# Gate products on half the rows of the array, low parts written over their source, and a later scaling in the final norm

## The chip, the cores and the metric

The kernel runs on one core of a Trainium2 chip. The metric is the device time of one launch in microseconds (us). Five engines work side by side, each through its own stream of instructions: TensorE (PE; its weight loads are shown as PEld), VectorE (DVE), ScalarE (ACT), GpSimd (POOL) and SyncE (SP), which issues the DMAs. An engine waits for another through semaphores.

## The reference

One decoder block on 2048 tokens of 1024 channels, all in float32:

```python
u = rms_norm(h, norm1_gain)
x_lru, g_lru, q, k, v, g_ret = split(u @ w_in)                  # 6 x 512 columns
xc = causal_depthwise_conv(x_lru)                               # width 4
r = sigmoid(einsum("bshi,hij->bshj", xc_by_head, wa) + ba)      # 8 heads of 64
i = sigmoid(einsum("bshi,hij->bshj", xc_by_head, wx) + bx)
a = exp(-8 * r * softplus(-lam))
hl = scan(h = a*h + sqrt(1 - a*a) * (i*xc))                     # RG-LRU
y_lru = rms_norm(hl * gelu(g_lru))
y_ret = head_norm(retention(rotary(q), rotary(k), v)) * silu(g_ret)   # 4 heads of 128
h = h + concat(y_lru, y_ret) @ w_out
up = causal_depthwise_conv(rms_norm(h) @ ffn_up_w)              # width 3, 2 x 3072 columns
a_branch, v_branch = split(up)
h = h + (gelu(a_branch) * v_branch) @ ffn_down_w
return rms_norm(h, final_norm_gain)
```

The two einsums are the gates: each of the 8 heads has its own 64x64 matrix for r and another for i.

## The kernel before

Channels lie on partitions and tokens on the free axis. A big product is made in three fp32r products instead of one fp32 product. Each operand x is split into a high part, which ScalarE rounds to fp32r (CAST; `bh` of the data, `wh` of the weights), and a low part x - high, which VectorE subtracts (`bl`, `wl`). TensorE then adds wh·bh + wh·bl + wl·bh. The large matrices are multiplied by a Strassen scheme: a `Unit` takes 2x2 blocks and makes seven products of 12 matmuls of 128x512; the first of the seven factors are sums of weight blocks (`s`, `s1`) that VectorE makes. A `PlainUnit` takes the eight plain products of a 2x2 scheme instead and needs no sums. The kernel has 745 such groups of 12 matmuls ("product blocks"); they fill PSUM banks named pq, px, py, pe.

The work runs in stages for two groups of 1024 tokens, g0 and g1: the input projection of g0 (its first units plain, on raw input, hence `RawStage`; then Strassen units) and of g1, with the gates, the scan and the retention among them until about 610 us; the output projection of both (plain); from about 815 us the up-projection of g0, then of g1, with its width-3 convolution (tiles `c`, `o`); and from about 1735 us the down-projection of both. `Stage.bring` loads a 512 KB block of data into a slot `raw`, splits it into two further slots and frees the raw one. SBUF is cut into 54 slots of 128x1024 floats.

The order of all instructions is worked out ahead by a planner (`Flow`): every piece of work is a Python generator that yields operations with a cost in us, a priority in ticks (one tick is about one product block's place), or a request for a slot or a PSUM bank. At each step the planner gives the engine that is free first the ready operation of best priority. `RESERVE` and `NEAR` hold slots back from work that is not due soon, `BACKLOG` bounds how far DMAs are issued ahead, and `WB`, `LESS`, `XD0`, `RAW` and `STAGE_LEAD` set when weight sums, the conversion of x, the split of blocks and their loads fall due. The engines then run the resulting fixed streams, each in its order.

Four pieces are named below. `LruOut.first` makes the gates of one 128-channel tile (two heads) for 1024 tokens: for each half of 512 tokens an fp32 matmul of the full 128x128 block-diagonal matrix into bank `pa` and another into `pg`, then two sigmoids by ACT. There are 8 such tiles (4 in each group), so 16 pairs of gate products. Banks `sm` (three of them) serve the gates and every other small product: scores `sc`, the retention state `pk`, transposes, row sums `mst` (ones times a sum of squares `sqacc`), broadcasts `pb`. `FinalGroup.piece` closes the last RMSNorm: the last pairs of output tiles arrive in token ranges of 512, 256 and 256 columns; when a range is complete, its power (`rstd`: mst, ms on DVE and POOL, pb, then the copy `rb` by ACT) is worked out, and eight scalings res·gain·rb by DVE follow, each with its output DMA.

Of the kernel before, what the change touches and what calls it, by code (L numbers as in the profile page):

```python
# [30 lines left out]
P = 128  # L31
# [11 lines left out]
RESERVE = 7  # L43
NEAR = 3
BACKLOG = 6.0
# [4 lines left out]
WB = 0  # L50
# [3 lines left out]
LESS = 2  # L54
XSTEP = 6
XD0 = 6
XS = 60
XD = 50
RAW = 4
LEAD = 10  # L60
STAGE_LEAD = 16
# [41 lines left out]
class Engine:  # L103
# [24 lines left out]
    def cost_pe(self, op, n, args, kw):  # L128
        if op == "transpose":
            return 0.13  # L130
        one = max(0.03, 0.0133 + n / 2400)
        return one if args[1].dtype == F32R else 4 * one
# [185 lines left out]
def hymba_block_kernel(ctx: ExitStack, tc: tile.TileContext, xh, xn, win, wout, wup, down, gates, vecs,  # L318
# [30 lines left out]
    def dma(dst, src):  # L349
        n = 1  # L350
        for d in dst.shape:
            n *= d
        return Op("sp", lambda: nc.sync.dma_start(dst, src), ISSUE, parts(dst), parts(src), kb=n / 256)
# [141 lines left out]

    class Stage:
# [19 lines left out]
        def bring(self, name, i, need, start):  # L516
            yield Until(start)
            r = yield Slot("raw")
            yield from self.src.get(r, name, i)
            yield need - 2  # L520
            self.blk[name, i] = yield from split(r, "b")
            free(r)
# [8 lines left out]
    class RawStage(Stage):  # L531
# [6 lines left out]
        def bring(self, name, i, need, start):  # L538
            k, n = int(name[0]) - 1, int(name[1]) - 1
            yield Until(start)  # L540
            r = yield Slot("raw")
            if self.gain is None:
                yield from self.src[2 * k + i].get_half(r, n)
# [4 lines left out]
            if self.gain is None:  # L548
                self.blk[name, i] = yield from split(r, "b")
# [8 lines left out]
            free(r)  # L558
# [483 lines left out]
    class LruOut(PlainOut):  # L1042
# [17 lines left out]
        def first(self):  # L1060
# [13 lines left out]
            gat = e[:, 0:2 * P].rearrange("p (a b) -> p a b", b=P)  # L1074
            yield dma(gat, gates[:, 2 * c:2 * c + 2])
# [4 lines left out]
            for n in range(2):  # L1080
                pa = yield Bank("sm", "pa")
                yield pe.matmul(pa, gat[:, 0], xc[:, half(n)], start=True, stop=True)
                px = yield Bank("sm", "pg")
                yield pe.matmul(px, gat[:, 1], xc[:, half(n)], start=True, stop=True)
                yield a.activation(t[:, half(n)], pa, AF.Sigmoid, bias=col(V_BA + c))
                free(pa)
                yield a.activation(gi[:, half(n)], px, AF.Sigmoid, bias=col(V_BX + c))
                free(px)
# [291 lines left out]
    class FinalGroup(NormGroup):  # L1380
# [6 lines left out]
        def piece(self, m, t, c0, c1):  # L1387
# [7 lines left out]
            if self.count % 2 == 0:  # L1395
                r = yield Slot("rb")
                r = r[:, 0:c1 - c0]
                yield from rstd(self.ss.acc, D, r, c0, c1)
                for k in range(KT):
# [4 lines left out]
        def out(self, k, y, c0, c1):  # L1404
            yield dma(yT[k * P:(k + 1) * P, HT * (NG - 1) + c0:HT * (NG - 1) + c1], y)
# [153 lines left out]
def _layout(inputs):  # L1559
# [26 lines left out]
    gates = np.zeros((P, 8, P), f32)  # L1586
    for c in range(4):
        for i, name in enumerate(("lru_gate_a_w", "lru_gate_x_w")):
# [40 lines left out]
```

## Time and profile before

| | |
|---|---|
| time, median of 3 runs | 2207.14 us (2205.99 to 2207.38) |
| the profiled execution's own time | 2206.14 us |
| its span in the trace | 2204.4 us (1.7 us lie outside it) |
| mean granted TensorE clock | 0.993 of full speed |
| busy: PE, DVE, ACT, POOL | 98%, 80%, 56%, 2% |
| TensorE's idle time in all | 33.7 us, of which 7.3 us stand behind its last instruction |

Busy shares are means over the whole span, and a busy TensorE can still run at half speed, so the idle gaps of TensorE, the engine that ended each, and the granted clock in the stretch behind it say more than the shares. Every operation is recorded by one helper line (L124), so rows are told apart by tile names. A matmul's duration in the trace overlaps that of the next; the distance between two starts is what each takes.

### The profile page before, as it was taken

How to read it: one execution, taken by the hardware profiler on the slowest of the kernel's cores; microseconds unless marked ns; L12 is line 12 of the kernel's file. 1: busy time of each engine (PE TensorE's matmuls, PEld its weight loads, DVE VectorE, ACT ScalarE, POOL GpSimd, SP SyncE). 2: the span in 40 equal slices, each digit the busy share in tenths (PEclk: the TensorE clock that was granted, in tenths of full speed). 3: DMA queues.
4: the chain of work that ended last, by engine and by line, in shares of the span. 5: the costliest groups of instructions: out<-in, count | busy, mean ns of one | idle time of the engine just before them, and what ended most of it. 6: DMA issues, size and time to landing. Idle time of an engine off the chain costs nothing.

```text
span 2204.4 us, 26724 instructions
## 1 busy us (share of the span) xinstructions
PE 2170.5 (98%) x9938; PEld 1793.2 (81%) x9938; DVE 1765.0 (80%) x2228; ACT 1224.0 (56%) x1763; POOL 42.0 (2%) x30
## 2 busy tenths in 40 slices
PE   9999999999999999999999999999999999999997
PEld 7877878888888788888888878888888788888886
DVE  6998888777764688898788897878788887797775
ACT  6674665565732266666666866666667544343441
POOL 0010010000000000000000000000000000000000
PEclk9999999999999999999999999999999999999999
DMA  9955464133664944444233532323236677689762
GB/s 345 358 200 191 124 224 157 60 112 103 204 234 177 376 188 143 169 152 161 90 108 126 210 120 84 122 90 110 96 101 217 246 283 274 226 304 345 274 231 77
DMA packets 140530, 408.36 MB, mean 185 GB/s; under 512 B 15728, under 2 KB 20208, under 8 KB 140400
## 3 DMA queue, kind: packets, MB, share of 16 engines
q1 hardware_dynamic: 140400, 406.65, 52.7%
q8 instruction: 78, 1.28, 0.2%
q14 instruction: 52, 0.43, 0.1%
HBM read 273.16 MB, written 125.04 MB: 181 GB/s over the span
## 4 chain that ended last, share of the span: by engine, by line
PE 93%; DVE 4%; DMA 1%; ACT 1%; issue 1%; POOL 0%; SPq 0%; POOLq 0%; DVEq 0%
PE py L124 33%; PE px L124 22%; PE pe L124 21%; PE pq L124 12%; PE po L124 1%; DMA raw<-in_dram 1%; PE sc L124 1%; PE pt L124 1%; PE pb L124 1%; PE pk L124 1%; PE pa L124 1%; PE pg L124 1%; DVE res L124 1%; PE mst L124 1%; DVE wl L124 0%
## 5 line engine op out<-in xcount | busy, mean ns | idle before, releaser
L124 PE MATMUL py<-bh,wh 128*128 128x512 f32 x728 | 288.1, 396 | 3.9 <-ACT wh L124 3.9
L124 PE MATMUL py<-bh,wl 128*128 128x512 f32 x728 | 285.5, 392 | 4.5 <-DVE wl L124 4.5
L124 PE MATMUL px<-bh,wh 128*128 128x512 f32 x728 | 287.7, 395 | 0.0
L124 PE MATMUL pe<-bl,wh 128*128 128x512 f32 x728 | 283.4, 389 | 1.8 <-DVE bl L124 1.8
L124 PE MATMUL py<-bl,wh 128*128 128x512 f32 x728 | 285.1, 392 | 0.0
L124 PE MATMUL px<-bh,wl 128*128 128x512 f32 x728 | 283.5, 389 | 1.6 <-DVE wl L124 1.6
L124 PE MATMUL pe<-bh,wh 128*128 128x512 f32 x728 | 285.0, 391 | 0.0
L124 PE MATMUL pe<-bh,wl 128*128 128x512 f32 x728 | 283.6, 390 | 0.1
L124 PE MATMUL px<-bl,wh 128*128 128x512 f32 x728 | 283.5, 389 | 0.0
L124 DVE TENSOR_TENSOR wl<-s,wh 128x1024 fp32r<-128x1024 f32 x182 | 222.1, 1220 | 71.3 <-ACT wh L124 71.0
L124 ACT CAST wh<-s 128x1024 fp32r<-128x1024 f32 x182 | 190.6, 1047 | 133.3 <-DVE s L124 119.2
L124 DVE SCALAR_TENSOR_TENSOR c<-o,vec,c 128x1022 f32<-128x1022 f32 x192 | 245.5, 1279 | 14.8 <-ACT c L124 9.3
L124 PE MATMUL py<-bh,wv 128*128 128x512 f32 x728 | 241.5, 392 | 1.0 <-DVE res L124 0.8
L124 ACT COPY o<-py 128x512 f32<-128x512 f32 x204 | 119.9, 588 | 199.5 <-PE py L124 196.4
L124 ACT CAST bh<-raw 128x1024 fp32r<-128x1024 f32 x158 | 162.9, 1050 | 54.7 <-DMA raw<-g 15.0
L124 DVE TENSOR_TENSOR bl<-raw,bh 128x1024 fp32r<-128x1024 f32 x158 | 189.3, 1218 | 4.3 <-ACT bh L124 3.2
L124 ACT ACTIVATE c<-o,vec 128x1024 f32<-128x1024 f32 x96 | 119.7, 1246 | 97.1 <-DVE o L124 95.6
L124 PE MATMUL pq<-bh,wh 128*128 128x512 f32 (+1 forms) x432 | 168.8, 391 | 1.3 <-ACT bh L124 1.2
L124 PE MATMUL pq<-bh,wl 128*128 128x512 f32 (+1 forms) x432 | 165.8, 384 | 1.5 <-DVE wl L124 1.5
L124 PEld LDWEIGHTS py<-bh,wl 128*128 128x128 f32 x728 | 137.7, 189 | 35.1 <-DVE wl L124 6.1
L124 PE MATMUL pq<-bl,wh 128*128 128x512 f32 (+1 forms) x432 | 165.5, 383 | 0.3 <-DVE bl L124 0.3
L124 PEld LDWEIGHTS py<-bh,wh 128*128 128x128 f32 x728 | 137.8, 189 | 33.3 <-ACT wh L124 4.7
(133 smaller groups left out, 3815.6 us busy)
## 6 DMA issues: line engine op xcount, KB each, us to landing
wa<-in_dram SPq DMA_DIRECT2D x91, 512.0 KB, 4.1
wb<-in_dram SPq DMA_DIRECT2D x91, 512.0 KB, 4.7
h<-res SPq DMA_DIRECT2D x56, 512.0 KB, 3.5
g_T<-t SPq DMA_DIRECT2D x96, 256.0 KB, 2.5
raw<-g_T SPq DMA_DIRECT2D x48, 512.0 KB, 6.3
res<-h SPq DMA_DIRECT2D x48, 512.0 KB, 6.2
g<-c SPq DMA_DIRECT2D x76, 256.0 KB, 3.1
raw<-g SPq DMA_DIRECT2D x38, 512.0 KB, 6.4
```

The costliest lines, as they stand in the source:

```text
L124: return Op(self.name, lambda: fn(*args, **kw), us, writes, reads, func=func)
```

## The change

Five edits. The gates of a tile are two products with 64 rows each, the first head's from rows 0 to 63 and the second head's from rows 64 to 127, into two banks, issued as one operation; each bank then holds r of one head and i of the other, and ACT reads four 64-row pieces instead of two of 128 rows. The low part of a data block is written over the raw block, in the slot that the load filled. The final norm's scalings get the lowest priority once the power is known. Half of the last outputs are issued by ACT's queue. Seven of the planner's constants have new values.

```diff
-RESERVE = 7
+RESERVE = 4
-BACKLOG = 6.0
+BACKLOG = 10.0
-WB = 0
+WB = 2
-LESS = 2
+LESS = 0
-XD0 = 6
+XD0 = 10
-RAW = 4
+RAW = 3
-STAGE_LEAD = 16
+STAGE_LEAD = 20
...
         one = max(0.03, 0.0133 + n / 2400)
+        if args[1].shape[0] == 64:
+            one /= 2
...
+    def split_here(raw, name):
+
+        hi = yield Slot(name + "h", F32R)
+        x = raw.bitcast(F32)
+        yield a.copy(hi, x)
+        yield low(raw, x, hi)
+        return hi, raw
...
         def bring(self, name, i, need, start):
             yield Until(start)
-            r = yield Slot("raw")
-            yield from self.src.get(r, name, i)
+            r = yield Slot("raw", F32R)
+            yield from self.src.get(r.bitcast(F32), name, i)
             yield need - 2
-            self.blk[name, i] = yield from split(r, "b")
-            free(r)
+            self.blk[name, i] = yield from split_here(r, "b")
...
-            gat = e[:, 0:2 * P].rearrange("p (a b) -> p a b", b=P)
-            yield dma(gat, gates[:, 2 * c:2 * c + 2])
+            gat = e[:, 0:P]
+            yield dma(gat, gates[:, c])
...
             for n in range(2):
+
                 pa = yield Bank("sm", "pa")
-                yield pe.matmul(pa, gat[:, 0], xc[:, half(n)], start=True, stop=True)
-                px = yield Bank("sm", "pg")
-                yield pe.matmul(px, gat[:, 1], xc[:, half(n)], start=True, stop=True)
-                yield a.activation(t[:, half(n)], pa, AF.Sigmoid, bias=col(V_BA + c))
-                free(pa)
-                yield a.activation(gi[:, half(n)], px, AF.Sigmoid, bias=col(V_BX + c))
-                free(px)
+                pb = yield Bank("sm", "pg")
+                yield (pe.matmul(pa, gat[0:64], xc[0:64, half(n)], start=True, stop=True) +
+                       pe.matmul(pb, gat[64:P], xc[64:P, half(n)], start=True, stop=True))
+                for dst, ps, bias in ((t, (pa, pb), V_BA), (gi, (pb, pa), V_BX)):
+                    for i in range(2):
+                        lo = 64 * i
+                        src = ps[i][lo:lo + 64] if dst is t else ps[1 - i][64 - lo:P - lo]
+                        yield a.activation(dst[lo:lo + 64, half(n)], src, AF.Sigmoid, bias=vec[lo:lo + 64, bias + c:bias + c + 1])
+                free(pa, pb)
...
                 yield from rstd(self.ss.acc, D, r, c0, c1)
+                yield 10 ** 5
                 for k in range(KT):
                     y = self.t[k][:, c0:c1]
                     yield v.scalar_tensor_tensor(out=y, in0=y, scalar=col(V_NF + k), in1=r, op0=ALU.mult, op1=ALU.mult)
                     fl.spawn(self.out(k, y, c0, c1), 10 ** 6)
...
         def out(self, k, y, c0, c1):
-            yield dma(yT[k * P:(k + 1) * P, HT * (NG - 1) + c0:HT * (NG - 1) + c1], y)
+            on_act = c0 > 0 and k % 2 == 1
+            yield dma(yT[k * P:(k + 1) * P, HT * (NG - 1) + c0:HT * (NG - 1) + c1], y, "a" if on_act else "sp")
```

The 745 product blocks follow one another in the same order in both kernels; what stands between them, and the order on DVE and ACT, differ. Three places follow, in which numbers behind a name tell one tile from another.

**Near 107 us of the run before (start of g0's second stage).** On VectorE of the kernel before, the low parts of the first px block's data (bl_849, bl_987) stand here:

```order
L124 TENSOR_TENSOR o1_677<-o1_677,sw_756 128x1024
L124 TENSOR_TENSOR o0_977<-pq_921,rb_563 128x512
L124 TENSOR_TENSOR bl_849<-raw_718,bh_750 128x1024
L124 TENSOR_TENSOR bl_987<-raw_719,bh_937 128x1024
L124 TENSOR_TENSOR o0_977<-pq_976,rb_563 128x512
L124 TENSOR_TENSOR wl_1040<-wa_978,wh_989 128x1024
L124 TENSOR_TENSOR s1_1003<-wb_982 128x512
L124 TENSOR_TENSOR s1_1003<-wa_978,wb_982 128x512
```

and on VectorE of the changed kernel its second low part (raw_634) stands here, st being the retention state and the pk small products of TensorE:

```order
L124 TENSOR_TENSOR raw_751<-raw_751,bh_952 128x1024
L124 TENSOR_TENSOR sg_1069<-sg_1069,o1_880 128x1024
L124 TENSOR_TENSOR wl_1164<-s1_987,wh_1141 128x1024
L124 SCALAR_TENSOR_TENSOR st_1156<-st_1156,pk_1158 128x128 x4
L124 SCALAR_TENSOR_TENSOR st_1156<-st_1156,pk_1184 128x128 x3
L124 SCALAR_TENSOR_TENSOR kT_925<-st_1156,pk_1184 128x128
L124 TENSOR_TENSOR raw_634<-raw_634,bh_1099 128x1024
L124 TENSOR_TENSOR raw_680<-raw_680,bh_1106 128x1024
```

TensorE of the changed kernel runs that px block directly behind the two pk:

```order
L124 MATMUL pk_1158<-vT_900,kT_925 128x128 x4
L124 MATMUL pk_1184<-vT_900,kT_925 128x128 x4
L124 MATMUL px_1154<-bh_844,wh_984 128x512
L124 MATMUL px_1154<-raw_633,wh_984 128x512
L124 MATMUL px_1154<-bh_844,wl_1038 128x512
L124 MATMUL px_1154<-bh_1099,wh_984 128x512
L124 MATMUL px_1154<-raw_634,wh_984 128x512
```

The second low part of the px block moved on VectorE from well ahead of the pk products to behind the updates that read them, and both pk moved ahead of the px block.

**Near 1279 us (border from the up-projection of g0 to that of g1).** VectorE before, from the last rows ahead of the low part of a summed weight block (wl_10324); bl_10260 is the data's last low part for that place:

```order
L124 SCALAR_TENSOR_TENSOR c_10188<-o0_10013,vec_69,c_10188 128x1022
L124 SCALAR_TENSOR_TENSOR c_10188<-o0_10013,vec_69,c_10188 128x1023
L124 TENSOR_TENSOR bl_10260<-raw_10093,bh_10185 128x1024
L124 TENSOR_TENSOR s1_10140<-s1_10140,wa_10090 128x512
L124 TENSOR_TENSOR c_10188<-c_10188,c_10145 128x1024
L124 TENSOR_TENSOR s1_10140<-wa_10090,s1_10140 128x512
L124 TENSOR_TENSOR t12_10318<-c_10017 128x512
L124 TENSOR_TENSOR o0_10184<-o0_10184,pe_10116 128x512
L124 TENSOR_TENSOR t12_10318<-c_10188,t12_10318 128x512
L124 TENSOR_TENSOR wl_10324<-s1_10140,wh_10321 128x1024
```

VectorE in the changed kernel, with the corresponding weights wl_10223 and the data's last low part raw_10108:

```order
L124 TENSOR_TENSOR raw_10037<-raw_10037,bh_10066 128x1024
L124 TENSOR_TENSOR s1_10071<-s1_10071,wa_10062 128x512
L124 TENSOR_TENSOR s1_10071<-wa_10062,s1_10071 128x512
L124 SCALAR_TENSOR_TENSOR c_10114<-o1_10032,vec_69,c_10114 128x1022
L124 SCALAR_TENSOR_TENSOR c_10114<-o1_10032,vec_69,c_10114 128x1023
L124 TENSOR_TENSOR wl_10223<-s1_10071,wh_10215 128x1024
L124 TENSOR_TENSOR o1_10191<-o1_10191,pe_10089 128x512
L124 TENSOR_TENSOR raw_10067<-raw_10067,bh_10110 128x1024
L124 SCALAR_TENSOR_TENSOR c_10171<-o0_9984,vec_69,c_10171 128x1022
L124 SCALAR_TENSOR_TENSOR c_10171<-o0_9984,vec_69,c_10171 128x1023
L124 TENSOR_TENSOR raw_10108<-raw_10108,bh_10111 128x1024
```

Before, the data's last low part stood seven rows ahead of the weights' low part; in the changed kernel it stands five rows behind it, and the weights' part comes ahead of the convolution's later rows.

**The end of the run.** VectorE before, from the middle of the first range's scalings (rb_17185) to the second range's:

```order
L124 SCALAR_TENSOR_TENSOR res_16864<-res_16864,vec_69,rb_17185 128x512
L124 SCALAR_TENSOR_TENSOR res_16991<-res_16991,vec_69,rb_17185 128x512
L124 TENSOR_SCALAR ms_17246<-mst_17247 128x2
L124 TENSOR_TENSOR res_16990<-res_16990,pq_17223 128x256
L124 TENSOR_TENSOR res_16991<-res_16991,pq_17263 128x256
L124 TENSOR_TENSOR sqacc_16868<-sqacc_16868,sqt_17299 128x256
L124 TENSOR_TENSOR sqacc_16868<-sqacc_16868,sqt_17304 128x256
L124 SCALAR_TENSOR_TENSOR res_16555<-res_16555,vec_69,rb_17245 128x256
```

VectorE in the changed kernel, where the first range's scalings carry rb_17059 and the second's rb_17119:

```order
L124 SCALAR_TENSOR_TENSOR res_16745<-res_16745,vec_69,rb_17059 128x512
L124 TENSOR_TENSOR res_16871<-res_16871,pq_17137 128x256
L124 SCALAR_TENSOR_TENSOR res_16871<-res_16871,vec_69,rb_17059 128x512
L124 TENSOR_TENSOR sqacc_16749<-sqacc_16749,sqt_17181 128x256
L124 SCALAR_TENSOR_TENSOR res_16443<-res_16443,vec_69,rb_17119 128x256
L124 SCALAR_TENSOR_TENSOR res_16603<-res_16603,vec_69,rb_17119 128x256
L124 TENSOR_SCALAR ms_17187<-mst_17188 128x2
L124 SCALAR_TENSOR_TENSOR res_16744<-res_16744,vec_69,rb_17119 128x256
L124 SCALAR_TENSOR_TENSOR res_16869<-res_16869,vec_69,rb_17119 128x256
```

The eight scalings of a range no longer stand in one piece: the last tiles' additions and the next range's power (ms) have been moved in between them.

## Rows read from the trace of the kernel before

**Rows 1.** The page, sections 1 and 4: busy time of each engine; the last chain.
```profile
PE 2170.5 (98%) x9938; PEld 1793.2 (81%) x9938; DVE 1765.0 (80%) x2228; ACT 1224.0 (56%) x1763; POOL 42.0 (2%) x30
...
PE 93%; DVE 4%; DMA 1%; ACT 1%; issue 1%; POOL 0%; SPq 0%; POOLq 0%; DVEq 0%
```

**Rows 2.** Timeline of PE; in brackets its idle time before, and who ended it.
```profile
154.91 0.50 PE L124 MATMUL px<-bh,wl 128*128 128x512 f32 x1 [1.61 <-DVE wl L124]
...
169.24 0.50 PE L124 MATMUL py<-bh,wl 128*128 128x512 f32 x1 [2.78 <-DVE wl L124]
...
320.41 3.57 PE L124 MATMUL mst<-ones,sqacc 128*128 128x1 f32 x16 [3.04 <-DVE sqacc L124]
...
1279.42 0.50 PE L124 MATMUL py<-bh,wh 128*128 128x512 f32 x1 [1.76 <-ACT wh L124]
...
1281.28 0.50 PE L124 MATMUL py<-bh,wl 128*128 128x512 f32 x1 [1.13 <-DVE wl L124]
...
1738.75 0.50 PE L124 MATMUL pe<-bl,wh 128*128 128x512 f32 x1 [1.80 <-DVE bl L124]
...
1742.29 0.80 PE L124 MATMUL py<-bh,wh 128*128 128x512 f32 x1 [2.09 <-ACT wh L124]
...
2195.90 1.22 PE L124 MATMUL pb<-idt,ms 128*128 128x128 f32 x4 [3.66 <-POOL ms L124]
```

**Rows 3.** Stretches: busy us (instructions) of PE, PEld, DVE, ACT, POOL; PEclk, DMA share, GB/s.
```profile
55.00:110.00 55.00, 55.00 (x252) 44.38 (x251) 50.01 (x58) 33.09 (x42) 0.00 (x0) 1.00 0.97 358
169.00:172.00 3.00, 2.77 (x8) 2.18 (x9) 2.97 (x4) 0.00 (x0) 0.00 (x0) 0.71 0.99 321
1230.00:1285.00 55.00, 52.11 (x229) 42.53 (x228) 50.96 (x57) 43.73 (x68) 0.00 (x0) 1.00 0.56 200
1742.00:1746.00 4.00, 3.07 (x6) 1.99 (x7) 4.00 (x6) 0.76 (x2) 0.00 (x0) 0.50 0.71 272
```

**Rows 4.** Timeline of PE around the first pair of gate products.
```profile
67.38 1.02 PE L124 MATMUL pa<-xc,ea 128*128 128x512 f32 x2
68.23 1.02 PE L124 MATMUL pg<-xc,ea 128*128 128x512 f32 x2
68.69 0.79 PE L124 MATMUL pq<-bh,wh 128*128 128x512 f32 x1
69.32 0.40 PE L124 MATMUL pq<-bl,wh 128*128 128x512 f32 x1
69.56 0.40 PE L124 MATMUL pq<-bh,wl 128*128 128x512 f32 x1
```

**Rows 5.** Tile pa (first gate's bank): its products and its reader; ns are min/median/max.
```profile
L124 PE MATMUL pa<-xc,ea x32: 590/591/604, 67.4 to 592.1; 128*128 128x512 f32 x32
L124 ACT ACTIVATE tt<-pa,vec x16: 687/688/710, 68.4 to 592.7; 128x512 f32<-128x512 f32 x16
```

**Rows 6.** Timeline of ACT near the start.
```profile
13.42 1.05 ACT L124 CAST wh<-w 128x1024 fp32r<-128x1024 f32 x1 [0.57 <-DMA w<-in_dram]
```

**Rows 7.** Timeline of DVE and then PE near 107, in the second stage.
```profile
111.12 1.25 DVE L124 SCALAR_TENSOR_TENSOR st<-st,pk 128x128 f32<-128x128 f32 x4 [2.52 <-PE pk L124]
...
114.75 0.29 DVE L124 SCALAR_TENSOR_TENSOR st<-st,pk 128x128 f32<-128x128 f32 x1
...
110.03 1.05 PE L124 MATMUL pk<-vT,kT 128*128 128x128 f32 x8
```

**Rows 8.** Timeline of DVE and then PE at the border from g1's second stage to output projection.
```profile
604.42 2.35 DVE L124 TENSOR_TENSOR_SCAN xc<-ea,hlast,gi 128x1024 f32<-128x1024 f32 x1
...
606.99 1.22 DVE L124 TENSOR_TENSOR xc<-xc,o 128x1024 f32<-128x1024 f32 x1
...
607.83 0.48 PE L124 MATMUL pq<-bh,wh 128*128 128x512 f32 x1
```

**Rows 9.** Timeline of DVE at the end of the run.
```profile
2191.75 3.26 DVE L124 SCALAR_TENSOR_TENSOR res<-res,vec,rb 128x256 f32<-128x256 f32 x8 [0.16 <-ACT rb L124]
...
2197.57 3.26 DVE L124 SCALAR_TENSOR_TENSOR res<-res,vec,rb 128x256 f32<-128x256 f32 x8 [2.49 <-ACT rb L124]
```

More of the change, by code (lines that the diff above doesn't have):

```diff
@@ L347, in blk, with dma @@
         return t[:, c * P:(c + 1) * P]
-    def dma(dst, src):
+    def dma(dst, src, queue="sp"):
         n = 1
@@ L352, in dma @@
             n *= d
-        return Op("sp", lambda: nc.sync.dma_start(dst, src), ISSUE, parts(dst), parts(src), kb=n / 256)
+        start = (nc.scalar if queue == "a" else nc.sync).dma_start
+        return Op(queue, lambda: start(dst, src), ISSUE, parts(dst), parts(src), kb=n / 256)
     class Dram:
@@ L540, in bring @@
             yield Until(start)
-            r = yield Slot("raw")
+            r = yield (Slot("raw", F32R) if self.gain is None else Slot("raw"))
             if self.gain is None:
-                yield from self.src[2 * k + i].get_half(r, n)
+                yield from self.src[2 * k + i].get_half(r.bitcast(F32), n)
             else:
@@ L548, in bring @@
             if self.gain is None:
-                self.blk[name, i] = yield from split(r, "b")
+                self.blk[name, i] = yield from split_here(r, "b")
             else:
@@ L557, in bring @@
                 self.blk[name, i] = (hi, lo)
-            free(r)
+                free(r)
             self.event(name, i).on = True
@@ L1585, in _layout @@
         cols(inputs["ret_norm_gain"]), cols(inputs["ffn_conv_w"]), cols(inputs["ffn_conv_b"])], axis=1)
-    gates = np.zeros((P, 8, P), f32)
-    for c in range(4):
-        for i, name in enumerate(("lru_gate_a_w", "lru_gate_x_w")):
-            w = np.asarray(inputs[name])[0]
-            gates[:64, 2 * c + i, :64] = w[2 * c]
-            gates[64:, 2 * c + i, 64:] = w[2 * c + 1]
+    wa, wx = (np.asarray(inputs[n])[0].transpose(1, 0, 2) for n in ("lru_gate_a_w", "lru_gate_x_w"))
+    gates = np.concatenate([np.concatenate([wa[:, 0::2], wx[:, 0::2]], axis=2),
+                            np.concatenate([wx[:, 1::2], wa[:, 1::2]], axis=2)])
     freq = f32(10000.0) ** (-np.arange(0, P, 2, dtype=f32) / f32(P))
```

## The prediction

> **What bounds the kernel now.** I read the page first: TensorE is busy for 98% of the span and has 93% of the last chain, VectorE 4% [rows 1]. So two things can move the time: work that leaves TensorE, and gaps in TensorE's stream. The second view is TensorE's own timeline, of which only the rows with an idle time in brackets count. Of its 33.7 us of idle time, 7.3 stand behind its last instruction; the large gaps of the middle are few, and nearly all end on VectorE: low parts of weights at 154.91, 169.24 and 1281.28, a sum of squares at 320.41, a data block at 1738.75. Two end on a rounding by ACT (1279.42, 1742.29), which itself waited for VectorE's weight sums [rows 2]. The third view is the table by stretches. Near such gaps VectorE is nearly full: 50.96 of 55 us around 1279, 4.00 of 4 behind 1742. It also shows the price of a gap beyond its length: behind the wait of 2.78 us the granted clock was 0.71 for 169 to 172, and 1742 to 1746 ran at 0.50, the 1.2 GHz level [rows 3]. ACT has room: 33.09 of 55 us in the stage of the gates [rows 3].
>
> The sum is made against the profiled execution, 2206.1 us (span 2204.4 plus 1.7 outside), which is 1.0 below the median of the runs. A change under 0.2%, 4.4 us, can hardly be told from none for this kernel.
>
> **Gates, TensorE.** Each fp32 product goes through the array as two passes: pa starts at 67.38, pg at 68.23, so a pass takes 0.425 us and a pair of products four, 1.70; the check is the next block, whose second matmul starts at 69.32, which is 67.38 + 1.70 + one spacing of 0.24 [rows 4]. The tile view has 32 passes of pa [rows 5], so 16 pairs, 27.2 us. Now the two products of a pair sit in different halves of the array. No row of before shows two such products. Bounds: if both run fully side by side, a pair takes 0.85 (-13.7 in all); if nothing overlaps, 1.70 (0); if each pair also empties the array on entry and on exit, it costs more. An emptying is the part of a matmul's duration that overlaps the next, 0.40 - 0.24 = 0.16 [rows 4], so two per pair make +5.1. I take the middle: the stream has pa's two passes ahead of pg's two, and if matmuls start in order, pa's second pass and pg's first share the array while the outer two run alone: three passes, 1.28, plus one emptying, 1.44. That is 0.26 less for each of 16 pairs: **-4.2**.
>
> On that the Trainium skill has two rules that pull apart. "TensorE: Matmul & The Clock Gate", Part 3, says that matmuls in different row groups start some 4 ns apart, yet start and end strictly in program order; by it alone the term would be -6.8 (three passes). "TensorEngine Tiling (Array Packing)", Tiling Modes, Key Properties, says that a change of tiling mode drains TensorE, which every pair does twice here. No row of before shows either.
>
> **Gates, ACT.** Two sigmoids of 0.69 us for 128x512 [rows 5] become four for 64x512. I price a 64-row one the same, since the columns stay, so ACT gets 32 x 0.69 = 22 us more. ACT's free 40% hides this [rows 3]; without that cover it would all count. What shows is the banks: a pair holds two of three sm banks until the fourth sigmoid, 2.75 us instead of about 1.4. The order has two places where the next pair stands only 13 matmuls (some 3 us) behind; both wait about half a us: **+1**.
>
> **Low parts over the raw block.** The same CAST and the same subtraction, so nothing by itself; the cover that it needs is none. The slot it saves, and the seven constants, act through the order.
>
> **Order, start.** The changed order loads 512 KB of weights ahead of two raw blocks. In the DMA-bound stretch 358 GB/s were moved [rows 3], so that is 1.5 us; ACT already waits for a weight load at 13.42 [rows 6], and part of the delay lies under the first twelve matmuls: **+0.9**.
>
> **Order, 107 to 175.** The low parts of weights that are late at 154.91 and 169.24 now stand 11.9 and 5.1 us of VectorE work earlier. Both gaps should go: 1.61 + 2.78 [rows 2], and with them the slow stretch behind (0.29 x 3 us in 169 to 172 [rows 3], about as much behind it): 6.1 us. Against it, the px block near 107 now follows two pk products directly, and its second low part stands behind the state's seven updates and kT: 1.25 for four updates, 0.95 for three more at the same price, 0.29, then 1.22 of its own [rows 7, 8], some 3.9 us with the first signal, against about 2.4 us of TensorE work (the second pk, 1.05 less its overlap with the next [rows 7], and seven matmuls of 0.23): a wait of about 1.5. A broadcast's copy on ACT stands behind three CASTs of 1.05 [rows 6]; part of it shows, 2. Sum **-2.5**, with bounds -6 (neither new wait) and +2 (each a block's width, 2.7, and no slow stretch saved).
>
> **Order, 320.** The row sum mst moves one block later, but its sum of squares moves later on VectorE too: 0, within 3 us either way (the gap of now is 3.04 [rows 2]).
>
> **Order, 607.** Now VectorE's scan ends at 606.77 and its product at 608.2; PE passes 607.83 without a wait [rows 8]. In the changed order two data low parts of that PE block stand behind the product: they end at 609.4 and 610.6 (1.2 each). The first is wanted at 608.15, so 1.3 us of waiting; the second is wanted six matmuls later and just fits. Then mst stands one block earlier while its sum stands two rows later: about 1 more. **+2.3** (0 to 5).
>
> **Order, 1279 and 1738.** At 1279 the weights' low part comes 8.7 us of VectorE work earlier, so 1.76 + 1.13 [rows 2] should go; the data's last low part comes 2.5 us later and leaves about 0.9: **-2**. At 1738 the same happens: the weights are 9.4 us earlier, so 2.09 [rows 2] and half of 3.07 us of slow PE work [rows 3] go; the data are 1.8 later, so the gap of 1.80 [rows 2] becomes about 3.5: **-1.9**. Bounds for each 0 and -4.
>
> **The end.** Now eight scalings (3.26 us [rows 9]) stand ahead of the last range's power, PE idles 3.66 for it [rows 2], and the last eight follow at 2197.57 after 2.49 of waiting [rows 9]. In the changed order ms stands ahead of six of them, 6 x 0.41 = 2.4 earlier, and these six fill VectorE's wait; a walk through the rows ends the scalings at 2199.1 instead of 2200.8. Half of the outputs go through ACT's queue, idle by then: 0.3 more. **-2** (-3 to 0).
>
> Sum: -4.2 + 1 + 0.9 - 2.5 + 0 + 2.3 - 2 - 1.9 - 2 = -8.4, so 2197.7; said as 2198.
>
> **Rivals.**
> (a) The halves run fully side by side: gates -13.7 instead of -4.2, **2188**. For it: nothing ties the two products together, their banks and rows differ. Against: pa's second pass stands between.
> (b) The change doesn't do what it says: passes follow one another and the array empties twice per pair, +5.1 instead of -4.2: **2207**, no difference to tell. For it: two shapes of product meet here that the kernel before never mixes. The Trainium skill's rule in "TensorEngine Tiling (Array Packing)", Tiling Modes, that a change of mode drains TensorE is half of this case; its other rule there, that tiles work independently, speaks against the other half.
> (c) Slower: the later due time of the data's low parts (RAW 4 to 3) makes VectorE late wherever a stage begins, at 107, 607, 760, 1279 and 1738, by a whole block more than my walk has, 2.7 us each: +13.6 on -8.4, **2211.3**. It decides for slower from 2.6 us each on. For it: VectorE is full in just these stretches, and a gap there has cost TensorE its clock [rows 3]. Against: the low parts that are late before are the weights', which come earlier.
>
> **How the numbers follow.** Forecast 0.50, (a) 0.22, (b) 0.16, (c) 0.12. The forecast alone spans 2192 to 2205: the distances of the order terms and of the end from their bounds, added as independent (root of the sum of squares), are 6 down and 7 up. The range 2184 to 2210 goes from (a) less 4 us of order terms to just short of (c), and leaves out about 0.15. Faster by over 0.2%: nearly all of the forecast (0.47) and (a), 0.69; within 0.2%: (b) and the forecast's rest, 0.19; slower: (c), 0.12.
>
> **What would show it.** Gates: the distance from pa's start to the next block's second start, less 0.24: 1.28 to 1.44 by my step, 0.85 by (a), above 1.70 by (b). Sigmoids of 64x512 at 0.69. No idle time on wl near 155, 169, 1279 and 1744; new gaps on VectorE of 1.6 near 107 and 1.3 near 608. The last scalings 1.7 us nearer to the end of the products than now. The prediction is wrong if a new gap above 3 us stands at a border, or if the 64-row sigmoids make ACT the engine that TensorE waits for in the gates' stage.

## The result and the profile after

The changed kernel takes 2191.05 us (median of 6, 2189.44 to 2195.17) against 2206.56 (median of 6) for the kernel before: a ratio of 0.9934, 95% interval [0.9921, 0.9947], so 0.66% faster. The prediction was 2198, in a range of 2184 to 2210, with 0.69 on faster. The sign and the range were right; the likeliest number was 7 us too high.

The page of the changed kernel, busy time and chain, to be held against [rows 1]:

```profile
PE 2159.5 (99%) x9938; PEld 1781.6 (81%) x9938; DVE 1767.8 (81%) x2228; ACT 1244.6 (57%) x1795; POOL 44.4 (2%) x30
...
PE 94%; DVE 2%; DMA 1%; ACT 1%; issue 1%; SPq 0%; POOL 0%; POOLq 0%; DVEq 0%
```

TensorE is busy 11 us less, VectorE about as long, ACT 20.6 us more. VectorE's share of the last chain fell from 4% to 2%.

TensorE's timeline after, the gaps that matter, to be held against [rows 2]:

```profile
112.35 0.50 PE L124 MATMUL px<-raw,wh 128*128 128x512 f32 x1 [1.34 <-DVE raw L124]
...
151.42 0.50 PE L124 MATMUL py<-bh,wh 128*128 128x512 f32 x1 [0.99 <-ACT o L124]
...
181.66 0.50 PE L124 MATMUL pe<-bh,wl 128*128 128x512 f32 x1 [2.26 <-DVE wl L124]
...
315.33 0.79 PE L124 MATMUL px<-raw,wh 128*128 128x512 f32 x1 [3.50 <-DVE raw L124]
...
588.38 0.50 PE L124 MATMUL py<-bh,wv 128*128 128x512 f32 x1 [1.40 <-ACT o L124]
...
1729.46 0.50 PE L124 MATMUL pe<-raw,wh 128*128 128x512 f32 x1 [1.55 <-DVE raw L124]
...
1990.70 0.50 PE L124 MATMUL py<-bh,wh 128*128 128x512 f32 x1 [2.44 <-DVE res L124]
...
2180.99 1.22 PE L124 MATMUL pb<-idt,ms 128*128 128x128 f32 x4 [1.27 <-POOL ms L124]
```

The gaps at 1279 are gone, the three near 1740 have become one, and the last range's broadcast waits 1.27 instead of 3.66 (the row sum ahead of it 1.51 instead of 0.34). New are those at 112, 151, 181, 588 and 1990. Near 320 one gap stands in place of another: 3.50 for a data block's low part instead of 3.04 for a sum of squares.

The stretches 313 to 320 and 1728 to 1735 after, columns as in [rows 3]:

```profile
313.00:320.00 7.00, 4.67 (x11) 3.71 (x12) 6.96 (x8) 6.52 (x8) 0.00 (x0) 0.56 0.22 78
1728.00:1735.00 7.00, 5.54 (x24) 4.61 (x25) 6.97 (x10) 1.06 (x1) 0.00 (x0) 1.00 0.27 106
```

Around the gap of 3.50 the clock is at 0.56 in the mean; before, it was 0.50 from 321 to 327. Behind 1729 it stayed at full speed, where the kernel before ran 1742 to 1746 at 0.50 [rows 3]. Of stretches at the 1.2 GHz level ahead of the last 25 us, the kernel before has 20.5 us (four), the changed one 10.2 (two).

TensorE's timeline after, around the first pair of gates, to be held against [rows 4]:

```profile
62.80 0.39 PE L124 MATMUL pq<-bh,wl 128*128 128x512 f32 x1
63.12 0.69 PE L124 MATMUL pa<-xc,ea 64*128 64x512 f32 x1
63.12 0.69 PE L124 MATMUL pg<-xc,ea 64*128 64x512 f32 x1
63.65 0.59 PE L124 MATMUL pa<-xc,ea 64*128 64x512 f32 x1
63.66 0.59 PE L124 MATMUL pg<-xc,ea 64*128 64x512 f32 x1
64.18 0.50 PE L124 MATMUL pq<-bh,wh 128*128 128x512 f32 x1
64.51 0.39 PE L124 MATMUL pq<-bl,wh 128*128 128x512 f32 x1
```

Both first passes start together, then both second passes. From the end of the product ahead (62.80 + 0.23) to the start of the one behind (64.51 - 0.23) it is 1.25 us, against 1.70 before: 0.45 x 16 = 7.2 us. One of the 16 pairs falls out: at 375 the second product starts 0.48 late, released by VectorE, and that pair saves nothing. So the saving is some 6.9.

VectorE at the end of the run, to be held against [rows 9]:

```profile
2179.82 0.16 DVE L124 TENSOR_SCALAR ms<-mst 128x2 f32<-128x2 f32 x1
2179.90 2.45 DVE L124 SCALAR_TENSOR_TENSOR res<-res,vec,rb 128x256 f32<-128x256 f32 x6
2182.65 3.25 DVE L124 SCALAR_TENSOR_TENSOR res<-res,vec,rb 128x256 f32<-128x256 f32 x8 [0.29 <-ACT rb L124]
```

The power's ms stands at 2179.82, ahead of six scalings, and the last eight wait 0.29 for their broadcast instead of 2.49.

**Where the 15.2 us of span went.** The 745 product blocks have one order in both kernels, so the distance between the starts of the same block in the two traces tells what was gained by then. Times of the kernel before; negative is gained:

| stretch | predicted | measured |
|---|---|---|
| start, to 50 | +0.9 | +1.1 |
| 50 to 650: gates, banks, 107 to 175, 320, 607 | -3.4 | -5.2 |
| 650 to 850, with the gap at 760 | 0 | -1.4 |
| 1250 to 1300 | -2 | -3.5 |
| 1700 to 1750 | -1.9 | -5.4 |
| 1950 to 2050 | 0 | +1.8 |
| behind the last products | -2 | -2.6 |
| sum | -8.4 | -15.2 |

### The profile page after: what moved, and what is told of

The parts are those of the page before. It is cut to its first block, busy times and chain, and to the rows that moved or that the text cites. A ratio compares the mean times of both kernels' runs of the same rounds, so it can differ in the third digit from the quotient of the medians.

```text
span 2189.1 us, 26790 instructions
## 1 busy us (share of the span) xinstructions
PE 2159.5 (99%) x9938; PEld 1781.6 (81%) x9938; DVE 1767.8 (81%) x2228; ACT 1244.6 (57%) x1795; POOL 44.4 (2%) x30
## 3 DMA queue, kind: packets, MB, share of 16 engines
q8 instruction: 78, 1.28, 0.2%
## 4 chain that ended last, share of the span: by engine, by line
PE 94%; DVE 2%; DMA 1%; ACT 1%; issue 1%; SPq 0%; POOL 0%; POOLq 0%; DVEq 0%
PE py L124 33%; PE px L124 22%; PE pe L124 22%; PE pq L124 12%; PE po L124 1%; PE pa L124 1%; PE pb L124 1%; PE sc L124 1%; PE pt L124 1%; PE pk L124 1%; DVE raw L124 0%; PE mst L124 0%; DVE res L124 0%; DMA h<-res 0%; DMA h<-h 0%
## 5 line engine op out<-in xcount | busy, mean ns | idle before, releaser
L124 PE MATMUL px<-raw,wh 128*128 128x512 f32 x728 | 284.1, 390 | 4.8 <-DVE raw L124 4.8
L124 PE MATMUL pe<-raw,wh 128*128 128x512 f32 x728 | 283.4, 389 | 1.5 <-DVE raw L124 1.5
L124 PE MATMUL py<-raw,wh 128*128 128x512 f32 x728 | 283.8, 390 | 0.0
L124 DVE SCALAR_TENSOR_TENSOR c<-o,vec,c 128x1022 f32<-128x1022 f32 x192 | 244.4, 1279 | 6.2
L124 DVE TENSOR_TENSOR raw<-raw,bh 128x1024 fp32r<-128x1024 f32 x158 | 188.8, 1218 | 3.3 <-ACT bh L124 3.3
L124 PEld LDWEIGHTS px<-bh,wh 128*128 128x128 f32 x728 | 136.8, 188 | 33.6 <-issue 2.8
L124 PEld LDWEIGHTS px<-raw,wh 128*128 128x128 f32 x728 | 137.0, 188 | 33.3 <-DVE raw L124 5.7
L124 PEld LDWEIGHTS py<-bh,wv 128*128 128x128 f32 x728 | 136.7, 188 | 33.3 <-ACT o L124 1.6
```

The lines of the kernel that those rows point to most:

```text
L124: return Op(self.name, lambda: fn(*args, **kw), us, writes, reads, func=func)
```

## The experiments

Ratios are to the kernel before, run on the same chip; the changed kernel has 0.9934. The runs were made on several chips, on which the kernel before took 2206.6 to 2208.3 us. So the difference between two rows is better taken from their ratios, times 2207 us, than from their medians.

| run | what | median us | ratio, 95% interval |
|---|---|---|---|
| g_full | changed, gate products over all rows | 2198.95 | 0.9955 [0.9943, 0.9968] |
| g_same | changed, both gate products in one half (every second head's gates come from the wrong rows) | 2204.49 (one run) | |
| g_twice | changed, each gate pair twice | 2205.72 (one run) | |
| gates_only | before + gates | 2239.97 | 1.0151 [1.0138, 1.0165] |
| g_wb | before + gates + WB 2 | 2208.45 | 1.0007 [0.9998, 1.0016] |
| c_wb | changed, WB 0 | 2212.38 | 1.0017 [1.0008, 1.0026] |
| split_old | changed, low parts in new slots | 2193.81 | 0.9937 [0.9924, 0.9951] |
| end_old | changed, end as before | 2191.64 | 0.9935 [0.9922, 0.9947] |
| gates_old | changed, gates as before | 2195.24 | 0.9938 [0.9926, 0.9951] |
| c_raw | changed, RAW 4 | 2210.89 | 1.0011 [1.0002, 1.0020] |
| h_later | changed, first group's last scalings later | 2190.83 | 0.9916 [0.9903, 0.9930] |
| quad | changed, gates in quarters, three sigmoids | 2194.60 | 0.9940 [0.9925, 0.9956] |

### What a pair of gate products costs: g_full, g_same, g_twice

```diff
 g_full: both products over 128 rows, the matrices padded with zeros, the planner's cost kept
-yield (pe.matmul(pa, gat[0:64], xc[0:64, half(n)], ...) +
-       pe.matmul(pb, gat[64:P], xc[64:P, half(n)], ...))
+both = (pe.matmul(pa, gat[:, 0], xc[:, half(n)], ...) +
+        pe.matmul(pb, gat[:, 1], xc[:, half(n)], ...))
+both.us /= 2
+yield both
 g_same: the second product reads the first one's rows
-       pe.matmul(pb, gat[64:P], xc[64:P, half(n)], ...))
+       pe.matmul(pb, gat[0:64], xc[0:64, half(n)], ...))
 g_twice: the pair is issued twice, the planner's cost kept
+both = []
+for again in range(2):
+    both.append(pe.matmul(pa, gat[0:64], ...) + pe.matmul(pb, gat[64:P], ...))
+us = both[0].us
+both = both[0] + both[1]
+both.us = us
+yield both
```

> The changed kernel, but both gate products of a pair run over all 128 rows, with zeros in the other head's rows; banks, the four sigmoids and the order on every engine stay those of the changed kernel. Theory (the gates' gain is local: a pair takes 1.25 us in the changed trace against 1.70 before, 16 times): 7.2 us slower than the changed kernel, 2198 us, pair spacing back at 1.70 us. Rival (the shorter pair only lets TensorE wait elsewhere, and most of the 15 us comes from the order): less than 3 us slower, 2191 to 2194.

> The changed kernel, but the second product of each pair is read from rows 0 to 63 as the first one is (so the gates of every second head are computed from the wrong rows). Theory (the two products share the array because they lie in different halves): they now queue, a pair takes four passes of 0.43 to 0.53 us, 1.8 to 2.2 us, and the kernel is 9 to 15 us slower than the changed one in its trace. Rival (64-row products overlap wherever they lie, or a 64-row pass is simply shorter): the pair stays at 1.25 us.

> The changed kernel, but each gate pair is issued twice in a row into the same banks, with the same values; the rest of the order is unchanged. It measures what a pair costs without the way in and out. Theory (0.53 us for a pass of both halves is the price of every pass in this form: 0.43 of streaming and 0.1 of not hidden weight load): the second pair adds 1.06 us, 17 us in all. Rival (the 0.1 is paid only where the array goes from 128 rows to 64 and back): the second pair adds 0.85 us, 13.7 in all.

All three keep the changed kernel's order on VectorE and ACT. g_full came out 7.9 us above the changed kernel by the medians, 4.6 by the ratios (0.0021 of 2207), and 4.2 at the last product of its trace. That lies between the theory's 7.2 and the rival's under 3, and the two intervals overlap a little, so the times don't decide between them. The trace does: in it each pair is back at 1.70, which makes 6.9 us, and some 3 us of that came back, as TensorE's gaps add up to 21.1 us instead of 22.4 and its stretches at 1.2 GHz ahead of the last 25 us to 6.8 instead of 10.2 (half of the 3.4 is lost time). g_same, TensorE's timeline around its first pair:

```profile
62.49 1.12 PE L124 MATMUL pa<-xc,ea 64*128 64x512 f32 x2
63.45 1.02 PE L124 MATMUL pg<-xc,ea 64*128 64x512 f32 x2
64.40 0.50 PE L124 MATMUL pq<-bh,wh 128*128 128x512 f32 x1
```

In one half the passes queue: 0.96 us from pa to pg and 0.95 on, and each pair costs 0.85 more than in the changed kernel (0.39 more for the pair at 375). By the last product that makes 13.3 us, inside the 9 to 15 that were expected. So it is the place in different halves that lets them overlap. g_twice, the second to last passes of its first double pair:

```profile
62.43 0.59 PE L124 MATMUL pa<-xc,ea 64*128 64x512 f32 x1
62.44 0.59 PE L124 MATMUL pg<-xc,ea 64*128 64x512 f32 x1
62.86 0.59 PE L124 MATMUL pa<-xc,ea 64*128 64x512 f32 x1
62.87 0.59 PE L124 MATMUL pg<-xc,ea 64*128 64x512 f32 x1
63.29 0.59 PE L124 MATMUL pa<-xc,ea 64*128 64x512 f32 x1
63.29 0.59 PE L124 MATMUL pg<-xc,ea 64*128 64x512 f32 x1
```

Inside, a pass of both halves takes 0.43 (62.43 to 62.86 to 63.29), as long as a pass of before. Each doubled pair costs 0.86 more, 13.8 for 16; at the last product of its trace it is 15.1 us behind, the rest in gaps. My theory (0.53 for every pass, 17 us) fell, the rival holds: the extra is paid once on the way in and once on the way out, 1.25 - 2 x 0.425 = 0.40 us for a pair. That the Trainium skill's page "TensorEngine Tiling (Array Packing)", Tiling Modes, Key Properties, says of a change of mode, that it drains TensorE, agrees with these rows. Its size is 0.40 us here, in and out together, where I had counted one emptying of 0.16.

### What the gates bring with and without the rest: gates_only, gates_old

```diff
 gates_only: the kernel before with the new LruOut.first, gate matrices and the line in cost_pe
+        if args[1].shape[0] == 64:
+            one /= 2
 gates_old: the changed kernel with LruOut.first and the gate matrices of before
```

> The kernel before with the gates of the change alone (64-row pairs, four sigmoids, the halved cost in the planner); constants, low parts and the end are those of before. Theory (gates local, and the order of before keeps its waits): 6 to 8 us faster than before, 2199 to 2201. Rival (the gates' gain needs the new constants; without them the four sigmoids hold the banks and make new waits): within 3 us of before.

> The changed kernel with the gates as before (two fp32 products over 128 rows, two sigmoids, the old matrices), all else as changed; the planner orders it anew. Theory (under the new constants the four sigmoids are hidden, so the gates' edit is worth its 7.2 us on TensorE): 2196 to 2201 us, as the full-row products with four sigmoids (2199). Rival (ACT's 22 us more work still cost waits under the new constants, so taking them away gives most of it back): 2189 to 2194 us.

gates_only missed both: the edit that shortens TensorE's work made the kernel 33 us slower (1.0151 of 2207). ACT's timeline of gates_only near 230, the first group's LRU:

```profile
229.32 0.68 ACT L124 ACTIVATE gi<-pg,vec 64x512 f32<-64x512 f32 x1
230.75 1.28 ACT L124 ACT_TABLE_LOAD   x1
232.05 1.16 ACT L124 ACTIVATE ea<-tt,m8sp 128x1024 f32<-128x1024 f32 x1
...
234.40 1.28 ACT L124 ACT_TABLE_LOAD   x1
...
236.66 1.03 ACT L124 CAST wh<-s 128x1024 fp32r<-128x1024 f32 x1
```

the same place in the kernel before:

```profile
229.91 1.05 ACT L124 CAST wh<-s 128x1024 fp32r<-128x1024 f32 x1 [0.48 <-DVE s L124]
...
234.87 1.06 ACT L124 CAST wh<-wa 128x1024 fp32r<-128x1024 f32 x1 [0.99 <-DMA m<-sg]
235.95 1.28 ACT L124 ACT_TABLE_LOAD   x1
```

and TensorE's timeline of gates_only there:

```profile
237.74 0.80 PE L124 MATMUL pe<-bh,wh 128*128 128x512 f32 x1 [4.41 <-ACT wh L124]
...
243.05 0.80 PE L124 MATMUL pe<-bh,wl 128*128 128x512 f32 x1 [4.09 <-DVE wl L124]
```

The last of the tile's sigmoids, then two loads of ACT's function tables of 1.28 each and the gates' further functions (rows ea and tt) now stand in one piece ahead of the CAST of the weights (236.66). In the kernel before, two such CASTs stand ahead of the first table load; so they do in the changed kernel (228.55 and 232.41, the table load at 233.48). In gates_only TensorE waits 4.41 for that CAST and 4.09 for the low part, which VectorE makes behind the scan. TensorE's gaps (those of 0.2 us and more) add up to 52.9 us against 26.4, and stretches at 1.2 GHz ahead of the end to 54.6 us against 20.5. Whether the two more sigmoids for each pair do this by their length, or the planner's other order by the two banks held together and the halved cost, no run separates.

With gates_old the other side is seen: without the gates' edit, but with all the rest, 2195.24, between the two expectations, and a ratio that can't be told from the changed kernel's. The traces give the balance. gates_old is 2.3 us behind at the last product; its pairs take the 6.9 us more, but its gaps are 4.7 us less (17.7 against 22.4), as those at 112, 151 and 181 don't stand in it, and its slow stretches ahead of the last 25 us are as long (10.2). So the saving on TensorE is real, and under the new constants two thirds of it go back into gaps that come with the new gates; alone, with the constants of before, they cost far more than it.

### Which of the rest pays: g_wb, c_wb, c_raw, split_old

```diff
 g_wb: gates_only with
-WB = 0
+WB = 2
 c_wb: the changed kernel with
-WB = 2
+WB = 0
 c_raw: the changed kernel with
-RAW = 3
+RAW = 4
 split_old: the changed kernel with new slots for both parts, in Stage.bring and likewise in RawStage
...
-            self.blk[name, i] = yield from split_here(r, "b")
+            self.blk[name, i] = yield from split(r, "b")
+            free(r)
```

> The kernel before with the gates of the change and one constant, WB = 2, which makes the weights' parts fall due two ticks earlier; everything else as before. The gates alone cost 32 us, in waits of TensorE for weights (and some data) near 238, 243, 327, 478, 554 and 636 us. Theory (the four sigmoids lengthen ACT's stretch ahead of the weights' rounding, and only the due time of the weights is missing): those waits go, 2196 to 2206 us. Rival (ACT's 22 us more work are the cause, and an earlier due time only moves the wait): still over 2220 us.

> The changed kernel with WB back at 0, the other six constants as changed. Theory (WB pays for the gates): 10 to 30 us slower than the changed kernel, 2201 to 2221 us, with gaps of TensorE that end on the weights' wh and wl in the stage of the gates. Rival (the slots saved by the low parts and the other constants suffice): within 4 us of the changed kernel.

> The changed kernel with RAW back at 4: the split of a data block falls due one tick (one product block, 2.7 us) earlier. Theory (the gaps on raw at 112, 315 and 1729 in the changed trace, 1.34 + 3.50 + 1.55, come from the later due time): these three go or shrink to half, 2185 to 2190 us. Rival (VectorE is full there; an earlier low part makes a weight or a sum late instead): within 3 us of the changed kernel or slower.

> The changed kernel with data blocks split into two new slots as before, all else as changed. Theory (the saved slot only acts through the order, and the 54 slots are not what limits): within 4 us of the changed kernel, 2187 to 2195. Rival (RESERVE 4, WB 2 and STAGE_LEAD 20 need the slots that the overwritten blocks give back): over 8 us slower, with gaps that end on late weights or on DMA.

One constant takes 32 us off gates_only (g_wb, 1.0007; its median is 2 us above the expected 2196 to 2206), and its absence costs the changed kernel 18 (c_wb; 21 by the medians). The three largest of TensorE's gaps in c_wb:

```profile
175.14 0.80 PE L124 MATMUL py<-bh,wl 128*128 128x512 f32 x1 [5.02 <-DVE wl L124]
...
473.20 0.80 PE L124 MATMUL py<-bh,wl 128*128 128x512 f32 x1 [3.89 <-DVE wl L124]
...
549.59 0.50 PE L124 MATMUL py<-bh,wl 128*128 128x512 f32 x1 [3.89 <-DVE wl L124]
```

All end on the weights' low part, none of them stands in the changed kernel. So with the new gates, making the weights earlier pays: both runs show that. What WB 2 does with the gates of before was not run. The other six constants, the low parts and the end together are worth the remaining 16 us between g_wb and the changed kernel. g_wb's gaps on data are longer (4.98 at 315, 6.41 at 614).

c_raw missed its theory widely: it is 17 us slower than the changed kernel (20 by the medians), on the side of its rival. In the kernel RAW is not the due time of the split, as the prediction and this expectation have it: a block's process starts with the priority need - RAW, which holds for its slot and its load, and the split behind them has need - 2 with either value. So RAW 4 lets data blocks take slots and loads one tick earlier, ahead of others. TensorE's two largest gaps in c_raw, then a row of VectorE:

```profile
320.98 0.80 PE L124 MATMUL px<-raw,wh 128*128 128x512 f32 x1 [5.69 <-DVE raw L124]
...
402.82 0.79 PE L124 MATMUL py<-bh,wl 128*128 128x512 f32 x1 [4.45 <-DVE wl L124]
...
311.87 1.23 DVE L124 TENSOR_TENSOR o<-o,rope 128x1024 f32<-128x1024 f32 x1 [3.12 <-DMA rope<-in_dram]
```

The gap on raw grew to 5.69, and a weight is late at 402, where the changed kernel waits for nothing. Ahead of the first, VectorE stands 3.12 us for the rotary table, whose two loads are issued in between those of data blocks (at 300.45 and 302.09). The changed kernel issues them ahead of these blocks (from 295.02), and VectorE doesn't wait for them. That fits what RAW sets, but no run moves the table's loads alone, and the constant makes the planner deal slots and rows anew from 10 us on. Which of the rows that came later made the 17 us was not settled.

The aligned traces tell where these runs part. From 50 to 650 us, the stage of the gates, the changed kernel gains 5.2 on the kernel before, gates_old 1.4 and split_old 0.5, while g_wb loses 9.3, c_raw 13.7, c_wb 18.8 and gates_only 30.5. At the two borders behind it the changed kernel, gates_old, split_old, c_wb and c_raw are much alike: 2.8 to 3.5 gained from 1250 to 1300, and 4.2 to 5.5 from 1700 to 1750; g_wb gains 2.2 and 1.9. So WB and RAW decide over the gates' stage. The gains at the borders stay with either of them set back. Which constant they come from is not shown, and the kernel before with the seven constants alone was not run.

split_old (0.9937) can't be told from the changed kernel. The overwritten low part as such is worth nothing that can be measured here, as expected.

### The end and the gap at 1990: end_old, h_later

```diff
 end_old:
-                yield 10 ** 5
...
-            on_act = c0 > 0 and k % 2 == 1
-            yield dma(yT[...], y, "a" if on_act else "sp")
+            yield dma(yT[...], y)
 h_later, in NormGroup.normed, between the loads and the scalings:
+            if self.keep and self.vcol == V_NF:
+                yield Until(fl.tick + 3)
```

> The changed kernel with the final norm and its outputs as before (scalings at the priority of their power, all outputs on SP's queue); the order ahead of the last 20 rows of VectorE is the same. Theory (the tail after the last product shrank by 3.1 us in the trace, and nothing ahead of it depends on it): 2.5 to 3.5 us slower than the changed kernel, and the idle time of TensorE ahead of the last broadcast is back at about 3.7. Rival (the earlier power is given back by the last scalings, and the 3 us come from the queue or the clock): under 1 us.

> The changed kernel, with each of the first group's last scalings (h times gain times rb, near 1977 to 1990 us) held back three ticks behind its load; TensorE's order is unchanged, VectorE's differs in some 14 places there. In the changed trace VectorE stands 3.88 and 2.88 us for these loads, and TensorE then waits 2.44 for an eviction queued behind them. Theory: the gap at 1990 goes, 2 to 4 us faster than the changed kernel, 2187 to 2189. Rival (the loads themselves fill the queue, and the wait moves to a weight or to a data block near 2000): within 1 us.

VectorE at the end of end_old:

```profile
2183.05 3.26 DVE L124 SCALAR_TENSOR_TENSOR res<-res,vec,rb 128x256 f32<-128x256 f32 x8 [2.49 <-ACT rb L124]
```

The wait of 2.49 is back, and from the last product to the end it takes 14.9 us instead of 11.8, as before (14.8); 0.4 of that difference is the second range's broadcast, which the changed kernel puts ahead of the last twelve products. So in the trace the end's edit is worth 2.6 us. The medians show 0.6, which is the rival's figure; the runs of the changed kernel spread over 5.7 us and those of end_old over 5.3, so the time can't confirm the trace's number. In the two traces the difference is lost ahead of the end, where both have the same order: end_old is 2.3 us ahead at the last product, 1.8 of them from the first 50 us and 1.5 from 1950 to 2050. So two executions of one order can differ by some 2 us.

VectorE in the changed kernel ahead of the new gap at 1990. The first row waits for a load of h that is to be scaled and written out, the second, a weight's low part, for a store of a residual block (h<-res). The expectation took both for loads:

```profile
1982.86 1.28 DVE L124 SCALAR_TENSOR_TENSOR h<-h,vec,rb 128x1024 f32<-128x1024 f32 x1 [3.88 <-DMA h<-h]
1987.02 1.23 DVE L124 TENSOR_TENSOR wl<-wa,wh 128x1024 fp32r<-128x1024 f32 x1 [2.88 <-DMA h<-res]
```

TensorE's row there in h_later:

```profile
1993.43 0.50 PE L124 MATMUL py<-bh,wh 128*128 128x512 f32 x1 [0.92 <-DVE res L124]
```

The gap fell from 2.44 to 0.92; VectorE now waits 3.40 for an output's store, ahead of the same low part. But other runs with the changed kernel's order at that place have less than 2.44 there too: 1.23 in end_old, 1.47 in g_twice, 1.56 in g_full, 1.94 in g_same. The median is 0.2 us below the changed kernel's, the ratio 0.9916 against 0.9934, with intervals that overlap. It is no slower; whether it is faster stays open.

### Quarters of the array: quad

```diff
-yield (pe.matmul(pa, gat[0:64], ...) + pe.matmul(pb, gat[64:P], ...))
...
+four = None
+for out, r0, c0 in ((pa, 0, 0), (pb, 64, 0), (pa, 64, 64), (pb, 0, 64)):
+    one = pe.matmul(out[c0:c0 + 64], gat[r0:r0 + 64, c0:c0 + 64], xc[r0:r0 + 64, half(n)], ...)
+    four = four + one if four else one
+four.us /= 2
+yield four
+yield a.activation(t[:, half(n)], pa, AF.Sigmoid, bias=col(V_BA + c))
...
 one sigmoid over 128 partitions for t; the two of gi stay
```

> The changed kernel, with each gate pair made as four products of 64 rows by 64 columns, one in each quarter of the array, so that one bank holds r of both heads in order and takes one sigmoid over 128 partitions; i of both heads lies with the heads swapped and takes two of 64. Same result, three sigmoids instead of four, 11 us less work for ACT; the planner orders it anew. Theory (quarters run side by side as the halves do, and the fourth sigmoid costs waits): a pair still takes 1.25 us, 2187 to 2191 us. Rival (two products in the same rows but other columns queue): a pair takes 2.1 us, 16 x 0.85 = 13.6 more, 2200 to 2206 us.

TensorE's timeline of quad around its first pair:

```profile
62.53 0.64 PE L124 MATMUL pa<-xc,ea 64*64 64x512 f32 x1
62.54 0.64 PE L124 MATMUL pg<-xc,ea 64*64 64x512 f32 x1
62.54 0.64 PE L124 MATMUL pa<-xc,ea 64*64 64x512 f32 x1
62.55 0.64 PE L124 MATMUL pg<-xc,ea 64*64 64x512 f32 x1
63.01 0.59 PE L124 MATMUL pa<-xc,ea 64*64 64x512 f32 x1
```

Four products of 64x64 start within 0.02 us and pass together, and a pair takes 1.21 us; the rival (columns queue) is out. Still the kernel is no faster (0.9940), and its 2194.60 lies above the theory's 2187 to 2191: by 200 us it is 7 us ahead of the changed kernel's trace, and by 350 it is 6 behind, with gaps of 1.94 at 206, 3.40, 1.22 and 2.35 between 313 and 326, and 17 us at 1.2 GHz from 312 on, 7 us in the changed kernel. Less work on ACT gave the planner another order, and by the traces that order lost at the border what had been gained by 200 us.

## Why the prediction was right, and where it was off

**The sign and the range** rest on reading gaps: which end on late weights, and that these weights stand earlier in the new order. That held at 155, 169, 1279 and 1742, where the named gaps are gone, though a new one of 2.26 on a weight stands at 181. One of the added waits came as placed, 1.34 at 112 (about 1.5 predicted). The start's +1.1 (+0.9 predicted) is no proof: other runs with the same order there have -0.1 (g_twice) to +1.8 (h_later) by 50 us. By its own words the prediction would be wrong if a new gap above 3 us stood at a border. One does, 3.50 at 315; it takes the place of the 3.04 that went, so the stretch from 300 to 350 lost only 0.9. At 607 the sum of squares costs 0.51, and the larger wait of 1.40 stands at 588 and ends on ACT.

**Gates on TensorE** were mis-sized, -4.2 for -6.9. The step that failed is "three passes, 1.28, plus one emptying, 1.44", with its condition "if matmuls start in order": the halves run fully side by side, two passes, as rival (a) has it, but the way in and out costs 0.40, more than the 0.16 that I took. Rival (a) alone would be 0.85 for a pair, rival (b) 1.70 or more; the truth, 1.25, is the pass count of the one with the emptying of the other, which (b) put at 0.32. What the Trainium skill's "TensorE: Matmul & The Clock Gate", Part 3, says of matmuls in other row groups starting some 4 ns apart agrees: in the two rows of the second passes the starts are 63.65 and 63.66. The start in strict program order that the prediction cites from the Trainium skill (same page and part) does not fit: g_same's code differs only in the rows that pg reads, and there both passes of pa run ahead of pg's, while here they alternate. If both streams have one order, the passes of one of the two kernels don't start in it; the profile doesn't show which.

**Gates on ACT**, "ACT's free 40% hides this" with +1 for banks, was the weakest step. In the changed kernel two thirds of the saving go back into gaps, and even that needs WB, which brings the weights' rounding forward: gates_only shows 33 us without it and the rest, c_wb 18. I named the cover, but took it from a mean over the stage and not from the rows of ACT ahead of a late weight. That it held here was luck: the same reasoning, put to gates_only, gave 6 to 8 us faster. Of the +1 for banks, a late start of 0.48 in one pair of 16 shows.

**1738** was mis-sized, -1.9 for -5.4. The data's wait did not grow to 3.5 but stayed at 1.55, and the whole slow stretch (6.8 us at half speed) went, not half of it. **1279**: -3.5 for -2, as the new wait of 0.9 on data did not come. **760**: I had no term for the gap of 1.46 that stands at 760.04 before and is gone.

**The gap at 1990** was missed: +1.8 net, a load and a store that VectorE waits for. It is not a term of the sum at all, since I looked for late rows of VectorE and not for late transfers.

**Rival (c)** put the danger in RAW 3, as a later due time of the low parts. RAW sets the slots and loads of the blocks, and the run with RAW 4 is 17 us slower, so both the premise and the sign of that argument were wrong.

**The total** was -8.4 for -15.2. Too small were the gates on TensorE by 2.7, 1738 by 3.5, 1279 by 1.5, 760 by 1.4 and the end by 0.6; against that stand 1990 with 1.8, the other terms of the gates' stage with 0.9 and the start with 0.2.

## What to carry to other kernels

Where a planner writes the order, price an edit with the rest of the constants at both settings: here the gates cost 33 us alone and make no difference beside the rest that the times can tell, and one constant for the weights' due time takes back 32 of the 33. A gap of TensorE can cost more than its length: 3 us of idle time at one border were worth 5.4 when they went, with the slow stretch behind them, while the gap of 2.44 at 1990 has no slow stretch behind it. And before less work on one engine is counted as a gain, look at what the same edit puts on the engine that feeds it.

## What the runs showed of the hardware

Products in the two halves of the array pass together even when each is two fp32 passes, and so do four in quarters. A pass of halves takes 0.43 us for 512 columns, as one over all rows; going from full-row products to halves and back costs 0.40 us once for a run of such passes, whether two or four follow one another in it. Sigmoids of 64 partitions take as long as those of 128 (0.68 and 0.69 us), so half the rows save ACT nothing.
